# Places in the partition: moving and loaded operand trade places (byte 0 and 64 modulo 128) at every change of matrix behind the first network

## The chip, the cores and the metric

The kernel runs on one core of one Trainium2 chip, as one program. The metric is the device time of one execution in microseconds (us); smaller is better. Before the change it is 989.61 us, the median of three runs (989.24 to 990.04).

## The reference

A decoder trunk of two layers works on 256 positions of 1024 float32 features. Each layer is a mixer between two gated feed-forward networks, each on a normalised copy of x and added to x. The mixer of the first layer is a gated MLP with a causal 128 x 128 mix of positions; that of the second is stick-breaking attention, whose keys and values come from x as it is ahead of the second layer.

```python
def swiglu(h, w_in, w_out):
    gu = h @ w_in
    gate, up = jnp.split(gu, 2, axis=-1)
    return (jax.nn.silu(gate) * up) @ w_out

for i in range(DEPTH):                      # DEPTH = 2, N_A = 1
    if i == N_A:
        kv = rms_norm(x, kv_norm) @ w_kv    # shared keys and values
    x = x + 0.5 * swiglu(rms_norm(x, ffn_norm[i, 0]), ffn_w_in[i, 0], ffn_w_out[i, 0])
    h = rms_norm(x, mix_norm[i])
    if i < N_A:
        x = x + chunked_sgu(h, ...)         # (u * (W_s LN(v) + b)) W_out, with u, v = gelu(h W_in)
    else:
        x = x + stick_breaking_attention(h @ b_w_q, k, v) @ b_w_o
    x = x + 0.5 * swiglu(rms_norm(x, ffn_norm[i, 1]), ffn_w_in[i, 1], ffn_w_out[i, 1])
return rms_norm(x, final_norm)
```

The hidden width of a network is 2816, that of the gated MLP 2048; there are 16 heads of 64 and 4 heads of keys and values.

## The kernel before

x is kept transposed (xT: 128 features in the partitions, 8 chunks, 256 positions). Every float32 operand of a large product is split into two float32r tiles, a high part and the rest, and `mm3` makes a product out of three matmuls: rest of a with high of b, high of a with rest of b, high with high. In a matmul, a is the operand loaded into TensorE (128 columns) and b the one that moves through it (256 columns, in the last out step 512). Each of the three matmuls has its own weight load. In the rows a matmul reads `out<-tile,tile`; wlo and whi are the rest and the high part of a piece of weights, and so on with l and h.

The stages, by the names of their PSUM tiles in the profile:

- Networks a, b, c and d (`ffn_in`, `ffn`). An in step computes 256 gate columns (ga, gb, gc, gd) and 256 up columns (ua to ud) with the weights loaded and the normalised x moving (xnh, xnl); 96 matmuls. An out step adds 256 hidden features (hh, hl) into y (ya, yb, yc); 48 matmuls with the weights loaded and h moving. 11 in and 11 out steps stand in turn, an out step two behind its in step; one of each make a period of 144 matmuls. Network d's out step (yo with hhd) is turned round: h is loaded and the weights move, 512 columns at a time.
- Between a and b the gated MLP: v (`project_rows`: xn loaded, weights moving), then the u loop: uu (weights loaded, xn moving), mix, ys (weights loaded, hhs moving).
- Between b and c the keys (kT) and the values (v again, from xk). Between c and d the attention: q, z, the transposes at, o, and yo with oT moving.

The weights come in by DMA from SP's queue in pieces of 128 x 1024, up to seven ahead. ScalarE rounds a piece into whi (line 85) and VectorE writes the rest into wlo (line 87). The pools hip and lop hold nine tiles each. A tile has 1056 elements per partition (4224 bytes), of which a piece takes 1024, from element `place` on: `W.add(source, place)`. Place 16 is 64 bytes. No order is written out for the networks beyond the loops; `ATT_STEPS` sets that of the attention.

The pools stand one behind the other in each partition, so tile sizes decide addresses. xnh and xnl are neighbours of 8192 bytes each; hh and hl are pools of four tiles of 2048 bytes. The bytes modulo 128 at which the operands of a step start:

| step | moving / loaded before | after |
|---|---|---|
| in step of a | 0 / 64 | 0 / 64 |
| out step of a | 64 / 0 | 64 / 0 |
| v | 64 / 0 | 0 / 64 |
| uu, in steps of b, c, d, q | 0 / 64 | 64 / 0 |
| ys, out steps of b and c, yo with oT | 64 / 0 | 0 / 64 |
| kT; values (v from xk) | 64 / 64; 64 / 64 | 64 / 0; 0 / 64 |
| z | 0 / 64 | 0 / 64 |
| o | 64 / 0 | 64 / 0 |
| out step of d | 0 / 64 | 0 / 64 |

Of the kernel before, what the change touches and what calls it, by code (L numbers as in the profile page):

```python
# [9 lines left out]
F32R = mybir.dt.float32r  # L10
# [5 lines left out]
P = 128  # L16
T = 256
D = 1024
KC = D // P
DFF = 2816  # L20
NPAIR = DFF // 256
DA = 2048
# [81 lines left out]
def trunk(  # L104
# [22 lines left out]
    out = out[0]  # L127
# [8 lines left out]
    act = ctx.enter_context(tc.tile_pool(name="act", bufs=1))  # L136
# [5 lines left out]
    hp = ctx.enter_context(tc.tile_pool(name="hp", bufs=4))  # L142
# [8 lines left out]
    def ybank(name):  # L151
        return py.tile([P, 512], F32, tag="py", name=name)

    def scratch(name, width=512):
        return scr.tile([P, width], F32, tag="scr", name=name, padded_shape=[P, 516])

# [21 lines left out]
    W = Weights(tc, rawp, hip, lop)  # L178

    def cols(w, c0, kh):  # L180
        return w[kh * 512 : (kh + 1) * 512, c0 : c0 + 256].rearrange("(k p) c -> p k c", p=P)

    def rows(w, r0):
        return w[r0 : r0 + P, :]

    def plan_in_out(n, ins, w_out):


        steps = {}
        for j in range(n + 1):  # L190
            if j < n:
                steps["in", j] = [[W.add(cols(w, c0 + 256 * j, kh)) for w, c0 in ins] for kh in range(2)]
            if j:
                steps["out", j - 1] = [W.add(rows(w_out, 256 * (j - 1) + P * m), 16) for m in range(2)]
        return steps

    def plan_ffn(i, s):
        return plan_in_out(NPAIR, [(ffn_w_in[i, s], 0), (ffn_w_in[i, s], DFF)], ffn_w_out[i, s])

    plan00 = plan_ffn(0, 0)  # L200
    plan_v = [[W.add(cols(a_w_in[0], DA + 256 * j, kh)) for kh in range(2)] for j in range(8)]
    plan_u = {}
    for step in U_STEPS:
        kind, j = step
        if kind == "in":
            plan_u[step] = [W.add(cols(a_w_in[0], 256 * j, kh)) for kh in range(2)]
        elif kind == "out":
            plan_u[step] = [W.add(rows(a_w_out[0], 256 * j + P * m), 16) for m in range(2)]
    plan01 = plan_ffn(0, 1)
    plan_kv = [[W.add(cols(w_kv, 256 * j, kh)) for kh in range(2)] for j in range(2)]  # L210
    plan10 = plan_ffn(1, 0)
    plan_q = [[W.add(cols(b_w_q[0], 256 * j, kh)) for kh in range(2)] for j in range(4)]
    plan_o = [W.add(rows(b_w_o[0], P * b), 16) for b in range(8)]
    plan11 = plan_ffn(1, 1)


    xin = {}
# [17 lines left out]
    for i, group in enumerate(ROWS):  # L235
        r0 = 0
        for name, ap in group:
            n = ap.shape[0]
# [32 lines left out]


    xT = act.tile([P, KC, T], F32, name="xT")
    xnh = act.tile([P, KC, T], F32R, name="xnh")
    xnl = act.tile([P, KC, T], F32R, name="xnl")
    acc = act.tile([P, T], F32, name="acc")
    rT = act.tile([P, 2], F32, name="rT")

# [4 lines left out]
    def prepare(d, gains, sq=True):  # L283

        for (name, i), h, l in gains:
            g = gain(name, i * KC + d)
            W.order(nc.scalar.activation(h[:, d, :], xT[:, d, :], AF.Copy, scale=g))
            W.order(
                nc.vector.scalar_tensor_tensor(  # L289
                    l[:, d, :], xT[:, d, :], g, h[:, d, :].bitcast(F32), ALU.mult, ALU.subtract  # L290
                )
            )
        if sq:
            square(d)
# [49 lines left out]
    def load_x(hf):  # L344

        for d in range(hf * 4, hf * 4 + 4):
            ptr = ybank(f"ptr{d}")
            for tt in range(2):
                W.order(
                    nc.tensor.transpose(  # L350
                        ptr[:, tt * P : (tt + 1) * P], xin[tt, hf][:, (d % 4) * P : (d % 4 + 1) * P], ident
                    )
                )
            if d % 2:
                W.order(nc.vector.tensor_copy(xT[:, d, :], ptr[:, :T]))
            else:
                W.order(nc.scalar.copy(xT[:, d, :], ptr[:, :T]))
        for d in range(hf * 4, hf * 4 + 4):
            prepare(d, [(("ffn", 0), xnh, xnl)], False)
            if d % 2 == 0:  # L360
                s = scratch(f"sqx{d}", T) if d else acc
                nc.gpsimd.tensor_mul(s, xT[:, d, :], xT[:, d, :])
                if d:
                    nc.gpsimd.tensor_add(acc, acc, s)
            if d == 2:
                W.piece = 512
                W.run_to(0, 1)
                W.piece = UNIT
        W.run_to(0, 2)
        for d in range(hf * 4 + 1, hf * 4 + 4, 2):  # L370
            square(d)
# [81 lines left out]
            if kh + 1 in mid:  # L453
                mid[kh + 1]()

    XN = (xnh, xnl)

    def ffn_in(tag, j, ids, mid={}, by_bank=False):

        banks = [gbank(f"g{tag}_{j}"), gbank(f"u{tag}_{j}")]  # L460
        project(banks, ids, XN, mid, by_bank)
        gs = scratch(f"gs{tag}_{j}")
        us = scratch(f"us{tag}_{j}")
        nc.vector.tensor_mul(pair(gs), pair(banks[0]), bc2(rb))
        nc.scalar.activation(gs, gs, AF.Silu)
        nc.vector.tensor_mul(pair(us), pair(banks[1]), bc2(rb))
        nc.vector.tensor_mul(us, us, gs)
        hh = hp.tile([P, 512], F32R, tag="hh", name=f"hh{tag}_{j}")
        hl = hp.tile([P, 512], F32R, tag="hl", name=f"hl{tag}_{j}")
        split(hh, hl, us)  # L470
        return hh, hl

# [56 lines left out]
    def spatial_bias(hf):  # L529
# [13 lines left out]
    norm = Rms("x")  # L543
    ffn(
        "a",
        plan00,
        [(("mix", 0), xnh, xnl)],
        {1: lambda: load_x(1), 3: norm.columns, 4: norm.rows},
        True,
        {  # L550
# [22 lines left out]
    norm = Rms("m0")  # L573
# [30 lines left out]
    def mix(j, u):  # L604
        bank = gbank(f"mix{j}")
        s = scratch(f"mx{j}")
        for m in range(2):
            c = 2 * j + m
            for n in range(2):
                nc.tensor.matmul(  # L610
                    bank[:, m * T + n * P : m * T + (n + 1) * P],
                    vsb[:, n, c * P : (c + 1) * P],
                    wsT[:, j, :],
                    start=True,
                    stop=True,
                )
            nc.vector.scalar_tensor_tensor(
                s[:, m * T : (m + 1) * T].rearrange("p (n t) -> p n t", n=2),
                bank[:, m * T : (m + 1) * T].rearrange("p (n t) -> p n t", n=2),
                gain("lng", c),  # L620
                bc2(bias[:, c, :]),
                ALU.mult,
                ALU.add,
            )
        nc.vector.tensor_mul(s, s, u)
        hh = hp.tile([P, 512], F32R, tag="hh", name=f"hhs{j}")
        hl = hp.tile([P, 512], F32R, tag="hl", name=f"hls{j}")
        split(hh, hl, s)
        return hh, hl

# [2 lines left out]
    y = Residual("s")  # L633
    tail = []
    for kind, j in U_STEPS:
# [4 lines left out]
        else:  # L640
            h = hs.pop(j)
            for m in range(2):
# [2 lines left out]
                    y.add(w, chunk(h, m), j == 0 and m == 0, False)  # L645
                else:
                    tail.append((w, chunk(h, m)))
    close(y, tail, 0, 1.0, [(("ffn", 1), xnh, xnl)])
    sgu.close()


# [3 lines left out]
    kz = [at.tile([P, 4, 2, T], F32R, name=f"kz{p}") for p in "hl"]  # L655
    vd = [at.tile([P, 2, 4, 2, 64], F32R, name=f"vd{p}") for p in "hl"]
    at.tile([P, 16], F32, name="gapx")
    xkh = at.tile([P, KC, T], F32R, tag="bigh", name="xkh")
    xkl = at.tile([P, KC, T], F32R, tag="bigl", name="xkl")
    for t in kz:  # L660
        nc.gpsimd.memset(t.bitcast(F32), 0.0)

    norm = Rms("f1")
    ffn("b", plan01, [(("kv", 0), xkh, xkl), (("ffn", 2), xnh, xnl)], {1: norm.columns, 2: norm.rows})


    XK = (xkh, xkl)
    bank = gbank("kT")
    norm = Rms("f2")
    project([bank], [[i] for i in plan_kv[0]], XK, {2: norm.columns})  # L670
# [17 lines left out]
        for r in range(2):  # L688
            split(vd[0][:, tt, :, r, :], vd[1][:, tt, :, r, :], src)

    ffn("c", plan10, [(("mix", 1), xnh, xnl)])
    zscale = [at.tile([P, 2], F32, name=f"zscale{n}") for n in "pn"]
    oT = [at.tile([P, KC, T], F32R, tag=f"big{p}", name=f"oT{p}") for p in "hl"]

    def q_out(j, bank):
        qh = hp.tile([P, 512], F32R, tag="hh", name=f"qh{j}")
        ql = hp.tile([P, 512], F32R, tag="hl", name=f"ql{j}")
        split(qh, ql, bank)
        return qh, ql

# [49 lines left out]
    def transposed(b, a):  # L750
        t0 = gbank(f"at0_{b}")
        t1 = gbank(f"at1_{b}")
        for h in range(2):
            nc.tensor.transpose(t0[:, h * T : h * T + P], a[0][:, h, :], ident)
            nc.tensor.transpose(t0[:, h * T + P : (h + 1) * T], a[1][:, h, :P], ident)
            nc.tensor.transpose(t1[:, h * P : (h + 1) * P], a[1][:, h, P:], ident)
        a0 = [hp.tile([P, 512], F32R, tag=f"h{p}", name=f"a0{p}{b}") for p in "hl"]
        a1 = [hp.tile([P, T], F32R, tag=f"a1{p}", name=f"a1{p}{b}", bufs=2) for p in "hl"]
        split(a0[0], a0[1], t0)
        split(a1[0], a1[1], t1[:, :T])  # L760
        return a0, a1
# [27 lines left out]
    y = None  # L789
# [24 lines left out]
    for step in ATT_STEPS.split():  # L814
        if step == "y":
            y = Residual("o")
        else:
            att_step(step[0], int(step[1]))
    close(y, tail, 0, 1.0, [(("ffn", 3), xnh, xnl)])
    att.close()  # L820


# [103 lines left out]
```

## Time and profile before

| | |
|---|---|
| median of three runs | 989.61 us |
| the profiled execution's own time | 990.2 us |
| its span, first to last instruction | 988.5 us |
| TensorE busy | 970.1 us, 8042 matmuls |
| weight loads busy | 950.6 us |
| VectorE / ScalarE / GpSimd busy | 642.8 / 503.5 / 85.5 us |
| mean granted TensorE clock | 0.995 |

Matmuls are pipelined: the duration of one in the profile (some 278 ns) is longer than the distance between the starts of two, so the pace is read from the starts in the timeline. Over a longer stretch it is the first start of the stretch, the first start behind it, and the count between. Where TensorE is busy without a break, a stage's time is its count of matmuls times that distance.

### The profile page before, as it was taken

Reading aid. Unit: us, or ns where it says so; the run is one execution under the profiler, and the core shown is the slowest. Engines: PE = TensorE matmul, PEld = TensorE weight load, DVE = VectorE, ACT = ScalarE, POOL = GpSimd, SP = SyncE. Lnnn points to the kernel's source line nnn. Section 1 sums busy time; section 2 is a strip of 40 time slices with the busy share of each in tenths; the row PEclk is TensorE's granted clock in tenths of the full one; section 3 lists DMA queues with packets and bytes.
Section 4 is the critical chain, followed back from the end, with each engine's and each line's share of the span. In section 5 each row is a group of like instructions: output and inputs, shape, how many; then the busy total and the mean of one; then the engine's idle time right before and its main releaser. Section 6 shows DMA issues by size and latency. Waiting matters only on the chain.

```text
span 988.5 us, 19306 instructions
## 1 busy us (share of the span) xinstructions
PE 970.1 (98%) x8042; PEld 950.6 (96%) x8042; DVE 642.8 (65%) x823; ACT 503.5 (51%) x690; POOL 85.5 (9%) x126
## 2 busy tenths in 40 slices
PE   9999999999999999999999999999998999999997
PEld 8999999999999999999999999999997899999996
DVE  6865666676866775656569665656678776555553
ACT  6644434575544563434358444444587675343433
POOL 4100000010000300000003000000156320000002
PEclk9999999999999999999999999999999999999999
DMA  9966565657555466666664856565643246656511
GB/s 293 335 204 194 178 189 188 192 161 222 176 188 172 129 203 194 196 194 195 191 195 144 251 180 202 182 207 178 193 155 96 92 132 210 195 188 199 186 43 43
DMA packets 135208, 179.56 MB, mean 182 GB/s; under 512 B 5624, under 2 KB 119376, under 8 KB 135120
## 3 DMA queue, kind: packets, MB, share of 16 engines
q1 hardware_dynamic: 134768, 177.76, 57.8%
q8 instruction: 63, 1.03, 0.4%
q0 software_dynamic: 192, 0.52, 0.2%
q14 instruction: 25, 0.20, 0.1%
q10 hardware_dynamic: 160, 0.05, 0.0%
HBM read 176.73 MB, written 1.05 MB: 180 GB/s over the span
## 4 chain that ended last, share of the span: by engine, by line
PE 88%; DVE 5%; ACT 2%; issue 1%; DMA 1%; POOL 1%; SPq 0%; ACTq 0%; POOLq 0%; DVEq 0%
PE yo L160 2%; PE yo L162 2%; PE yo L161 2%; PE gc L162 2%; PE uc L162 2%; PE gb L160 2%; PE gc L161 2%; PE gc L160 2%; PE uc L161 2%; PE gb L162 2%; PE gb L161 2%; PE ub L162 2%; PE uc L160 2%; PE ub L161 2%; PE ub L160 2%; PE ud L162 2%
## 5 line engine op out<-in xcount | busy, mean ns | idle before, releaser
L85 ACT CAST whi<-raw 128x1024 fp32r<-128x1024 f32 (+1 forms) x333 | 342.4, 1044 | 379.1 <-issue 194.3
L87 DVE TENSOR_TENSOR wlo<-raw,whi 128x1024 fp32r<-128x1024 f32 (+1 forms) x333 | 401.6, 1223 | 193.9 <-ACT whi L85 193.0
L302 POOL TENSOR_TENSOR acc<-acc,sq 128x256 f32<-128x256 f32 x39 | 33.6, 863 | 378.2 <-ACT sq L301 376.3
L160 PE MATMUL ga<-xnh,wlo 128*128 128x256 f32 x176 | 49.9, 283 | 0.0
L160 PE MATMUL ua<-xnh,wlo 128*128 128x256 f32 x176 | 48.8, 277 | 0.5 <-DVE wlo L87 0.5
L161 PE MATMUL ga<-xnl,whi 128*128 128x256 f32 x176 | 49.1, 279 | 0.2 <-DVE xnl L289 0.2
L160 PE MATMUL ya<-hha,wlo 128*128 128x256 f32 x176 | 48.9, 278 | 0.2 <-DVE xT L411 0.2
L160 PE MATMUL yc<-hhc,wlo 128*128 128x256 f32 x176 | 48.9, 278 | 0.1
L160 PE MATMUL gb<-xnh,wlo 128*128 128x256 f32 x176 | 49.0, 278 | 0.0
L160 PE MATMUL gd<-xnh,wlo 128*128 128x256 f32 x176 | 48.9, 278 | 0.0
L160 PE MATMUL yb<-hhb,wlo 128*128 128x256 f32 x176 | 48.9, 278 | 0.0
L162 PE MATMUL ga<-xnh,whi 128*128 128x256 f32 x176 | 48.9, 278 | 0.0
L160 PE MATMUL gc<-xnh,wlo 128*128 128x256 f32 x176 | 48.9, 278 | 0.0
L162 PE MATMUL gc<-xnh,whi 128*128 128x256 f32 x176 | 48.8, 277 | 0.0
L162 PE MATMUL uc<-xnh,whi 128*128 128x256 f32 x176 | 48.8, 277 | 0.0
L161 PE MATMUL gc<-xnl,whi 128*128 128x256 f32 x176 | 48.7, 277 | 0.0
L162 PE MATMUL gd<-xnh,whi 128*128 128x256 f32 x176 | 48.7, 277 | 0.0
L162 PE MATMUL gb<-xnh,whi 128*128 128x256 f32 x176 | 48.7, 277 | 0.0
L162 PE MATMUL ud<-xnh,whi 128*128 128x256 f32 x176 | 48.7, 277 | 0.0
L161 PE MATMUL gb<-xnl,whi 128*128 128x256 f32 x176 | 48.7, 277 | 0.0
L162 PE MATMUL ua<-xnh,whi 128*128 128x256 f32 x176 | 48.7, 277 | 0.0
L161 PE MATMUL uc<-xnl,whi 128*128 128x256 f32 x176 | 48.7, 277 | 0.0
(289 smaller groups left out, 3345.3 us busy)
## 6 DMA issues: line engine op xcount, KB each, us to landing
raw<-in_ffn_w_in_dram SPq DMA_DIRECT2D x176, 512.0 KB, 4.7
raw<-in_ffn_w_out_dram SPq DMA_DIRECT2D x88, 512.0 KB, 4.2
raw<-in_a_w_in_dram SPq DMA_DIRECT2D x32, 512.0 KB, 4.5
raw<-in_a_w_out_dram SPq DMA_DIRECT2D x16, 512.0 KB, 3.3
raw<-in_b_w_q_dram SPq DMA_DIRECT2D x8, 512.0 KB, 4.6
raw<-in_b_w_o_dram SPq DMA_DIRECT2D x8, 512.0 KB, 4.1
raw<-in_w_kv_dram SPq DMA_DIRECT2D x4, 512.0 KB, 4.2
xin<-in_x_dram SPq DMA_DIRECT2D x4, 256.0 KB, 4.9
```

The costliest lines, as they stand in the source:

```text
L85: ins = nc.scalar.copy(hi[:, cc], raw[:, cc])
L87: ins = nc.vector.tensor_sub(lo[:, cc], raw[:, cc], hi[:, cc].bitcast(F32))
L160: nc.tensor.matmul(o, al, bh, start=first, stop=False, skip_group_check=True)
L161: nc.tensor.matmul(o, ah, bl, start=False, stop=False, skip_group_check=True)
L162: nc.tensor.matmul(o, ah, bh, start=False, stop=last, skip_group_check=True)
L302: nc.gpsimd.tensor_add(acc, acc, s)
```

## The change

Only the addresses of tiles change. Network a keeps its places. Behind it the weights of each matrix, and the operands that they meet, are placed so that a step's moving operand starts at the half (byte 0 or 64 modulo 128) at which the moving operand of the step before it did not; z, o and their neighbours excepted, as the table above shows. For this the tiles of xn, xk, oT and h get 32 elements (128 bytes) more, so that they can start at element 0 or 16: xnh and xnl, which `placed` cuts twice (XA for network a, XN behind it), xk and oT, and the h tiles that `hidden` hands out. So the distance from xnh to xnl goes from 8192 to 8320 bytes, those from xkh to xkl and from oTh to oTl likewise, and that between neighbouring h tiles from 2048 to 2176 bytes; from hh to hl of one step it is 8704 instead of 8192. All that lies behind moves along. No instruction is added, taken away or moved on any engine, and no wait.

```diff
+    def hidden(tag, name, n=0):
+
+        return hp.tile([P, 512 + 32], F32R, tag=tag, name=name)[:, n : n + 512]
...
-    def plan_in_out(n, ins, w_out):
+    def plan_in_out(n, ins, w_out, at_in, at_out):
...
-                steps["in", j] = [[W.add(cols(w, c0 + 256 * j, kh)) for w, c0 in ins] for kh in range(2)]
+                steps["in", j] = [[W.add(cols(w, c0 + 256 * j, kh), at_in) for w, c0 in ins] for kh in range(2)]
...
-                steps["out", j - 1] = [W.add(rows(w_out, 256 * (j - 1) + P * m), 16) for m in range(2)]
+                steps["out", j - 1] = [W.add(rows(w_out, 256 * (j - 1) + P * m), at_out) for m in range(2)]
...
+    plan00 = plan_ffn(0, 0, 0, 16)
+    plan_v = [[W.add(cols(a_w_in[0], DA + 256 * j, kh), 16) for kh in range(2)] for j in range(8)]
...
-            plan_u[step] = [W.add(cols(a_w_in[0], 256 * j, kh)) for kh in range(2)]
+            plan_u[step] = [W.add(cols(a_w_in[0], 256 * j, kh), 16) for kh in range(2)]
...
-            plan_u[step] = [W.add(rows(a_w_out[0], 256 * j + P * m), 16) for m in range(2)]
...
+            plan_u[step] = [W.add(rows(a_w_out[0], 256 * j + P * m)) for m in range(2)]
+    plan01 = plan_ffn(0, 1, 16, 0)
+    plan_kv = [[W.add(cols(w_kv, 256 * j, kh), 16) for kh in range(2)] for j in range(2)]
+    plan10 = plan_ffn(1, 0, 16, 0)
+    plan_q = [[W.add(cols(b_w_q[0], 256 * j, kh), 16) for kh in range(2)] for j in range(4)]
+    plan_o = [W.add(rows(b_w_o[0], P * b)) for b in range(8)]
+    plan11 = plan_ffn(1, 1, 16, 16)
...
-    xnh = act.tile([P, KC, T], F32R, name="xnh")
-    xnl = act.tile([P, KC, T], F32R, name="xnl")
+    xnb = [act.tile([P, KC * T + 32], F32R, name=f"xn{p}") for p in "hl"]
+
+    def placed(n, ts=xnb):
+
+        return tuple(t[:, n : n + KC * T].rearrange("p (k t) -> p k t", k=KC) for t in ts)
+
+    XA = placed(0)
+    XN = placed(16)
...
-        project(banks, ids, XN, mid, by_bank)
+        project(banks, ids, XA if tag == "a" else XN, mid, by_bank)
...
-        hh = hp.tile([P, 512], F32R, tag="hh", name=f"hh{tag}_{j}")
-        hl = hp.tile([P, 512], F32R, tag="hl", name=f"hl{tag}_{j}")
+        hh, hl = (hidden(f"h{p}", f"h{p}{tag}_{j}", 16 if tag in "bc" else 0) for p in "hl")
...
+        hh, hl = (hidden(f"h{p}", f"h{p}s{j}", 16) for p in "hl")
...
-    xkh = at.tile([P, KC, T], F32R, tag="bigh", name="xkh")
-    xkl = at.tile([P, KC, T], F32R, tag="bigl", name="xkl")
+    XK = placed(0, [at.tile([P, KC * T + 32], F32R, tag=f"big{p}", name=f"xk{p}") for p in "hl"])
...
-    oT = [at.tile([P, KC, T], F32R, tag=f"big{p}", name=f"oT{p}") for p in "hl"]
+    oT = placed(16, [at.tile([P, KC * T + 32], F32R, tag=f"big{p}", name=f"oT{p}") for p in "hl"])
...
+        qh, ql = (hidden(f"h{p}", f"q{p}{j}") for p in "hl")
...
-        a0 = [hp.tile([P, 512], F32R, tag=f"h{p}", name=f"a0{p}{b}") for p in "hl"]
+        a0 = [hidden(f"h{p}", f"a0{p}{b}") for p in "hl"]
```

## Rows read from the trace of the kernel before

**Rows 1.** The page: busy engines, granted clock by slices, chain by engine.
```profile
PE 970.1 (98%) x8042; PEld 950.6 (96%) x8042; DVE 642.8 (65%) x823; ACT 503.5 (51%) x690; POOL 85.5 (9%) x126
...
PEclk9999999999999999999999999999999999999999
...
PE 88%; DVE 5%; ACT 2%; issue 1%; DMA 1%; POOL 1%; SPq 0%; ACTq 0%; POOLq 0%; DVEq 0%
```

**Rows 2.** Windows by stage, all engines; the first line names the columns.
```profile
core 0: us, PE busy (x) PEld busy (x) DVE busy (x) ACT busy (x) POOL busy (x), PEclk, DMA share, GB/s
36.00:186.00 150.00, 150.00 (x1309) 148.85 (x1308) 94.14 (x112) 64.44 (x72) 0.00 (x0) 1.00 0.66 202
197.00:244.00 47.00, 46.84 (x398) 46.59 (x397) 31.53 (x47) 29.70 (x45) 4.95 (x5) 1.00 0.61 185
340.00:522.00 182.00, 182.00 (x1597) 181.79 (x1596) 114.14 (x137) 88.70 (x114) 6.55 (x9) 1.00 0.62 190
535.00:715.00 180.00, 180.00 (x1575) 179.78 (x1574) 113.09 (x127) 83.39 (x101) 4.16 (x9) 1.00 0.67 205
715.00:796.00 81.00, 73.25 (x547) 69.12 (x547) 63.84 (x95) 58.60 (x114) 36.62 (x63) 0.96 0.35 111
```

**Rows 3.** Timeline, TensorE: network a's change from in to out (start us, us).
```profile
136.77 0.28 PE L160 MATMUL ya<-hha,wlo 128*128 128x256 f32 x1
136.88 0.28 PE L161 MATMUL ya<-hla,whi 128*128 128x256 f32 x1
...
139.49 0.28 PE L160 MATMUL ya<-hha,wlo 128*128 128x256 f32 x1
```

**Rows 4.** Timeline, TensorE: the v projection around 216 us and its end.
```profile
215.83 0.28 PE L160 MATMUL v<-whi,xnl 128*128 128x256 f32 x1
...
216.17 0.28 PE L160 MATMUL v<-whi,xnl 128*128 128x256 f32 x1
216.29 0.28 PE L161 MATMUL v<-wlo,xnh 128*128 128x256 f32 x1
...
216.76 0.28 PE L162 MATMUL v<-whi,xnh 128*128 128x256 f32 x1
...
244.42 0.28 PE L160 MATMUL uu<-xnh,wlo 128*128 128x256 f32 x1
```

**Rows 5.** Timeline, TensorE: network a's change from out to in.
```profile
159.43 0.28 PE L160 MATMUL ga<-xnh,wlo 128*128 128x256 f32 x1
...
159.79 0.28 PE L160 MATMUL ga<-xnh,wlo 128*128 128x256 f32 x1
```

**Rows 6.** Timeline, TensorE: first matmuls of two in steps of network b.
```profile
369.42 0.28 PE L160 MATMUL gb<-xnh,wlo 128*128 128x256 f32 x1
...
500.32 0.28 PE L160 MATMUL gb<-xnh,wlo 128*128 128x256 f32 x1
```

**Rows 7.** Timeline, TensorE: starts in the in steps of network c.
```profile
563.05 0.28 PE L160 MATMUL gc<-xnh,wlo 128*128 128x256 f32 x1
...
568.75 0.28 PE L160 MATMUL gc<-xnh,wlo 128*128 128x256 f32 x1
...
694.64 0.28 PE L160 MATMUL gc<-xnh,wlo 128*128 128x256 f32 x1
```

**Rows 8.** Groups of matmuls by line and shape, TensorE.
```profile
L160 PE MATMUL ga<-xnh,wlo 128*128 128x256 f32 x176 | 49.9, 283 | 0.0
...
L160 PE MATMUL uu<-xnh,wlo 128*128 128x256 f32 x128 | 35.5, 277 | 0.0
...
L160 PE MATMUL yo<-oTh,wlo 128*128 128x256 f32 x64 | 18.4, 294 | 0.3
L160 PE MATMUL q<-xnh,wlo 128*128 128x256 f32 x64 | 17.9, 280 | 0.0
```

**Rows 9.** Timeline, TensorE: the last network's out step (512 columns).
```profile
838.13 0.39 PE L160 MATMUL yo<-whi,hld 128*128 128x512 f32 x1
...
840.90 0.39 PE L160 MATMUL yo<-whi,hld 128*128 128x512 f32 x1
```

More of the change, by code (lines that the diff above doesn't have):

```diff
@@ L191, in plan_in_out, with plan_ffn @@
             if j < n:
-                steps["in", j] = [[W.add(cols(w, c0 + 256 * j, kh)) for w, c0 in ins] for kh in range(2)]
+                steps["in", j] = [[W.add(cols(w, c0 + 256 * j, kh), at_in) for w, c0 in ins] for kh in range(2)]
             if j:
-                steps["out", j - 1] = [W.add(rows(w_out, 256 * (j - 1) + P * m), 16) for m in range(2)]
+                steps["out", j - 1] = [W.add(rows(w_out, 256 * (j - 1) + P * m), at_out) for m in range(2)]
         return steps
[L197 to L201, printed above, removed]
+    def plan_ffn(i, s, at_in, at_out):
+        return plan_in_out(
+            NPAIR, [(ffn_w_in[i, s], 0), (ffn_w_in[i, s], DFF)], ffn_w_out[i, s], at_in, at_out
+        )
+    plan00 = plan_ffn(0, 0, 0, 16)
+    plan_v = [[W.add(cols(a_w_in[0], DA + 256 * j, kh), 16) for kh in range(2)] for j in range(8)]
     plan_u = {}
@@ L205, in trunk @@
         if kind == "in":
-            plan_u[step] = [W.add(cols(a_w_in[0], 256 * j, kh)) for kh in range(2)]
+            plan_u[step] = [W.add(cols(a_w_in[0], 256 * j, kh), 16) for kh in range(2)]
         elif kind == "out":
-            plan_u[step] = [W.add(rows(a_w_out[0], 256 * j + P * m), 16) for m in range(2)]
[L209 to L214, printed above, removed]
+            plan_u[step] = [W.add(rows(a_w_out[0], 256 * j + P * m)) for m in range(2)]
[5 more added lines that the diff above has]
+    plan11 = plan_ffn(1, 1, 16, 16)
     xin = {}
@@ L358, in load_x @@
         for d in range(hf * 4, hf * 4 + 4):
-            prepare(d, [(("ffn", 0), xnh, xnl)], False)
+            prepare(d, [(("ffn", 0), *XA)], False)
             if d % 2 == 0:
@@ L454, in project_rows @@
                 mid[kh + 1]()
-    XN = (xnh, xnl)
     def ffn_in(tag, j, ids, mid={}, by_bank=False):
         banks = [gbank(f"g{tag}_{j}"), gbank(f"u{tag}_{j}")]
-        project(banks, ids, XN, mid, by_bank)
+        project(banks, ids, XA if tag == "a" else XN, mid, by_bank)
         gs = scratch(f"gs{tag}_{j}")
@@ L546, in trunk @@
         plan00,
-        [(("mix", 0), xnh, xnl)],
+        [(("mix", 0), *XN)],
         {1: lambda: load_x(1), 3: norm.columns, 4: norm.rows},
@@ L625, in mix @@
         nc.vector.tensor_mul(s, s, u)
-        hh = hp.tile([P, 512], F32R, tag="hh", name=f"hhs{j}")
-        hl = hp.tile([P, 512], F32R, tag="hl", name=f"hls{j}")
+        hh, hl = (hidden(f"h{p}", f"h{p}s{j}", 16) for p in "hl")
         split(hh, hl, s)
@@ L647, in trunk @@
                     tail.append((w, chunk(h, m)))
-    close(y, tail, 0, 1.0, [(("ffn", 1), xnh, xnl)])
+    close(y, tail, 0, 1.0, [(("ffn", 1), *XN)])
     sgu.close()
@@ L663, in trunk @@
     norm = Rms("f1")
-    ffn("b", plan01, [(("kv", 0), xkh, xkl), (("ffn", 2), xnh, xnl)], {1: norm.columns, 2: norm.rows})
-    XK = (xkh, xkl)
+    ffn("b", plan01, [(("kv", 0), *XK), (("ffn", 2), *XN)], {1: norm.columns, 2: norm.rows})
     bank = gbank("kT")
@@ L689, in trunk @@
             split(vd[0][:, tt, :, r, :], vd[1][:, tt, :, r, :], src)
-    ffn("c", plan10, [(("mix", 1), xnh, xnl)])
+    ffn("c", plan10, [(("mix", 1), *XN)])
     zscale = [at.tile([P, 2], F32, name=f"zscale{n}") for n in "pn"]
-    oT = [at.tile([P, KC, T], F32R, tag=f"big{p}", name=f"oT{p}") for p in "hl"]
+    oT = placed(16, [at.tile([P, KC * T + 32], F32R, tag=f"big{p}", name=f"oT{p}") for p in "hl"])
     def q_out(j, bank):
-        qh = hp.tile([P, 512], F32R, tag="hh", name=f"qh{j}")
-        ql = hp.tile([P, 512], F32R, tag="hl", name=f"ql{j}")
+        qh, ql = (hidden(f"h{p}", f"q{p}{j}") for p in "hl")
         split(qh, ql, bank)
@@ L818, in trunk @@
             att_step(step[0], int(step[1]))
-    close(y, tail, 0, 1.0, [(("ffn", 3), xnh, xnl)])
+    close(y, tail, 0, 1.0, [(("ffn", 3), *XN)])
     att.close()
```

## The prediction

> **What bounds the kernel now.** I read the busy shares first, then the stretches, then the timeline of single matmuls. TensorE is busy 98% of the 988.5 us, the chain that ended last is 88% TensorE, and its granted clock is 9 (90% or more) in every slice, so it stands at the upper of its two levels, 2.4 GHz [rows 1]. By stretch it is busy in all of networks a, b and c, and in 46.84 of 47.00 us of the v projection; the attention leaves idle time (busy 73.25 of 81.00 us) [rows 2]. In the networks a to c VectorE and ScalarE stand below 65% there and the DMA share at two thirds. So time is the number of matmuls times the distance from one start to the next, and a change of addresses can do only one thing that counts: alter that distance.
>
> The distance is not the same everywhere. A matmul of 256 columns and its weight load go in step, and the rows show two spacings at the same clock and shape. In the first network's out step, 24 matmuls from 136.77 to 139.49 us take 2.72 us, 113.3 ns each [rows 3]. In the v projection, 240 matmuls from 216.17 to 244.42 us take 28.25 us, 117.7 ns each [rows 4]. No wait shows in either. I call them the short and the long spacing. In network c, 48 matmuls from 563.05 to 568.75 take 118.75 ns each [rows 7]: long spacing with another pattern.
>
> **What switches between them.** I set the start addresses of the built program beside the starts in the timeline, modulo 256 bytes, and looked at each matmul that follows at least five short spacings. Where its moving operand goes on at the place where the last one started (difference 0), the short spacing stays, for thousands of matmuls, even when the loaded operand jumps by 128 at every third one. Where the moving operand jumps by +64 (every in-to-out change of networks a to c: xn at 128, h at 192), it stays too, 30 times of 30; [rows 3] show one. Where it jumps by -64 (out-to-in, 192 back to 128), the next distances are long at every such change; [rows 5] show one, three matmuls from 159.43 to 159.79, 120 ns each. It comes back after some 4 to 48 matmuls, at a change of loaded tile. Where it jumps by 128, the spacing goes long too: this happens from the first network into v and at 216.17 us, the only place where v had short spacing. There the moving operand goes from the whi tile to its wlo tile, 38016 bytes = 148.5 x 256 further, at 216.29; the three matmuls from 215.83 to 216.17 took 113 ns each, the four from 216.29 to 216.76 117.5 [rows 4]. In the v stage 12 of 16 pairs of weight tiles have this jump of 128 between hi and lo at two of every three matmuls, and none of the 12 holds the short spacing; in the last network's out step (weights moving too) 12 matmuls of 512 columns from 838.13 to 840.90 us take 230.8 ns each, above twice 113.3 = 226.7 [rows 9].
>
> **The change, part by part.** No instruction, wait or order changes on any engine; only addresses do.
>
> 1. *Trading the halves (byte 0 and 64).* Within each step moving and loaded operand stood 64 apart and still do. By itself this turns the sign of the jumps at stage borders, a matter of some matmuls per border. Bounds: nothing, to 41 borders (11+11+11 network steps, 8 of the u loop) x 12 matmuls x 4.4 ns = 2.2 us either way; I take 0.
>
> 2. *xn's two tiles get 32 elements more.* This is the part that I think counts. xnh and xnl stood 8192 bytes = 32 x 256 apart; now it is 8320 = 32.5 x 256. Every in-projection streams xnh, xnl, xnh (lines 160 to 162), so two of every three of its matmuls now start with the moving operand 128 off modulo 256. In the built program such jumps rise from 430 to 3795. It holds for network a too, though its places are untouched. To the engine this is what v has today: two jumps of 128 in each triple, with moving and loaded operand an odd multiple of 64 apart.
> Count: 8 x 176 + 128 + 64 per line, three lines: 4800 matmuls (gates, ups, uu, q) [rows 8]. Price: they now run at a mixture. Eight periods of network b (1152 matmuls, 369.42 to 500.32) take 113.63 ns per matmul [rows 6], eight of c 114.23 (563.05 to 694.64) [rows 7]; mean 113.93; with the out third of a period at 113.3, its in part stands at (3 x 113.93 - 113.3) / 2 = 114.25. If none keeps the short spacing, they go to between 117.7 (v) and 118.75 (c's long stretch, whose loaded operand jumps as here). I take the middle, 118.2: 4800 x 3.95 ns = +19.0 us; ends +16.6 and +21.6. No trace shows an in-projection with this jump, so the lower end for a partial effect stays open, below as a rival.
>
> 3. *oT and xk widen in the same way.* 192 matmuls of the attention's output projection [rows 8], 4.3 ns: +0.8 us; bounds 0 (they lie partly beside the attention's idle time [rows 2]) and 0.9. kT and the kv values, 96 matmuls, had both operands at the same half; now opposite, but with the jump: 0, bounds -0.4 to +0.1.
>
> 4. *h tiles widen by 128 bytes.* hh and hl of one step are 4 x 2176 = 34 x 256 apart, so the out steps get no jump inside. But they are now entered from an in step with long spacing. Bounds: 0 to all 1968 matmuls (33 network out steps and 8 of ys, 48 each) long, x 4.4 = +8.7 us. Every long stretch that I followed ended at a change of loaded tile (c's at 568.75 after 48; uu after 24), and half of the entries are now jumps of +64, the harmless kind; I take +2.5.
>
> 5. *v and the last network's out step* keep their moving jumps from hi to lo weights: 0; v's loaded xn now jumps too, 0 to 384 x 1.05 ns (118.75 against 117.7) = +0.4; I take 0.
>
> 6. *ScalarE, VectorE, DMA*: same shapes, same counts; covered by TensorE, which in the networks never waits for them.
>
> Sum: 19.0 + 0.8 + 2.5 = +22.3 us. The profiled execution took 990.2 us (span 988.5); 1012.5. The median of the three runs, 989.6, is 0.6 below it, so I predict **1012 us**.
>
> **A rule weighed.** The Trainium skill (SBUF — State Buffer, "Who interferes with whom") gives TensorE two independent SBUF read ports and says that it never waits on anyone; TensorE: Matmul & The Clock Gate, "Step-by-step: what each phase is for", says that loading the next weights takes no read bandwidth from the running matmul. By it places would not matter and the time would stay at 989.6. The trace disagrees already: 117.7 against 113.3 ns at the same shape and clock.
>
> **Rivals.**
> - *No effect* (989.6 +- 1): the spacing depends on something other than addresses, for instance on which operand is the weights; v is long because its weights move, and xn's jump is harmless. For it: of the v and kv stages with moving weights nearly all are long, and jump and role come together in this trace. Against it: the one short stretch in v broke at a jump, at 216.17, and the four tile pairs of v without a jump include the only short one. Chance 0.09.
> - *Trading cures* (faster): a change of place at every border resets the step. Then v (entered so far without a trade) falls to 113.3: 8 blocks of 48 x 4.4 ns = 1.7 us; kT and values 96 x 5 = 0.5; the last network's out step, some 240 x 4.1 = 1.0; together -3.2, 986.4. It decides from the first border, network a into v: starts 113.3 ns apart behind some 200 us show it. Against it: borders with a trade go long at -64 today, and uu, entered with a trade, began with 24 long ones. Chance 0.06.
> - *Partial*: the jump breaks the spacing, but in some tile pairs it comes back, as for the -64 kind; half of the in matmuls long: 4800 x 2 ns = +9.5, 1000. Chance 0.07.
> - *Forecast*: 0.78; its own range is 1006 (16.6 alone) to 1021 (21.6 + 0.9 + 8.7).
>
> **Numbers.** The range must hold 8 in 10: the forecast's own and the partial case (1000, with 2 us below it), 998 to 1021; I leave out no effect and the cure (0.15) and the tails. A measurement of this kernel tells about 0.2% (2 us) from no change. Slower: forecast and partial, 0.85. Same: no effect, and a third of the cure, 0.10. Faster: 0.05.
>
> **What would show it.** Right: in networks a to d the in matmuls start 117.7 to 119 ns apart from the first tile to the last, the mean duration in the rows of ga and uu rises from 277 to 283 ns [rows 8] to 280 or more, network a slows as well although its places are unchanged; a period of b (144 matmuls) takes 16.8 us or more against 16.36. v stays near 117.7. Wrong: gb and gc still at 113.3 behind an xnl matmul; then the jump of the moving operand is not the cause. If only b to d slow and a doesn't, it is the traded halves (part 1) and not the widening (part 2).

## The result and the profile after

The change makes the kernel slower, by 1.8%: 1007.58 us, median of 5 runs (1007.13 to 1009.30), against 989.54 us of the kernel before, timed beside it (5 runs, 989.24 to 990.04). The ratio is 1.0185, 95% interval 1.0173 to 1.0197. The profiled execution took 1009.3 us, its span is 1007.6. The forecast was 1012, with a range of 998 to 1021.

From the page after: busy engines, granted clock by slices, chain by engine; they answer to [rows 1].
```profile
PE 987.2 (98%) x8042; PEld 967.4 (96%) x8042; DVE 643.6 (64%) x823; ACT 503.6 (50%) x690; POOL 86.0 (9%) x126
...
PEclk9999999999999999999999999999999999999999
...
PE 89%; DVE 5%; ACT 2%; issue 1%; DMA 1%; POOL 1%; SPq 0%; ACTq 0%; POOLq 0%; DVEq 0%
```

Nothing in them looks like a new bottleneck. The matmuls are as many, VectorE and ScalarE have the same busy times within a microsecond, the clock stands at the same level, and the chain is TensorE's. Only TensorE's busy times have grown: the matmuls' from 970.1 to 987.2 us, the weight loads' from 950.6 to 967.4. The windows by stage (the first line names the columns; the limits moved along with the stages) answer to [rows 2]:
```profile
core 0: us, PE busy (x) PEld busy (x) DVE busy (x) ACT busy (x) POOL busy (x), PEclk, DMA share, GB/s
36.00:186.00 150.00, 150.00 (x1276) 148.85 (x1276) 92.27 (x110) 62.96 (x72) 0.00 (x0) 1.00 0.64 200
197.00:247.00 50.00, 49.85 (x422) 49.43 (x421) 34.48 (x55) 32.05 (x52) 6.59 (x7) 1.00 0.62 190
347.00:533.00 186.00, 186.00 (x1591) 185.80 (x1590) 113.59 (x136) 88.04 (x112) 5.72 (x7) 1.00 0.59 185
546.00:731.00 185.00, 185.00 (x1583) 184.81 (x1583) 114.16 (x130) 84.35 (x105) 5.09 (x11) 1.00 0.65 198
```

TensorE is busy without a break in networks a to c as before, but gets through fewer matmuls in the same time: in 150 us of network a 1276 where it was 1309. So the pace has to be read from single starts. Timeline of TensorE, network a, the change from an out to an in step (start and duration in us), beside [rows 5]:
```profile
180.37 0.28 PE L164 MATMUL ga<-xnh,wlo 128*128 128x256 f32 x1
180.49 0.28 PE L165 MATMUL ga<-xnl,whi 128*128 128x256 f32 x1
180.61 0.28 PE L166 MATMUL ga<-xnh,whi 128*128 128x256 f32 x1
180.72 0.28 PE L164 MATMUL ga<-xnh,wlo 128*128 128x256 f32 x1
```

Three matmuls take 0.35 us, 117 ns each, and unlike before this does not pass: here are the starts of one in step of network b, of its next out step and the next in step, and of the in step eight periods later; then two of network c that lie eight periods apart. They answer to [rows 6] and [rows 7].
```profile
375.69 0.28 PE L164 MATMUL gb<-xnh,wlo 128*128 128x256 f32 x1
...
387.00 0.28 PE L164 MATMUL yb<-hhb,wlo 128*128 128x256 f32 x1
...
392.57 0.28 PE L164 MATMUL gb<-xnh,wlo 128*128 128x256 f32 x1
...
510.17 0.28 PE L164 MATMUL gb<-xnh,wlo 128*128 128x256 f32 x1
...
574.10 0.28 PE L164 MATMUL gc<-xnh,wlo 128*128 128x256 f32 x1
...
708.47 0.28 PE L164 MATMUL gc<-xnh,wlo 128*128 128x256 f32 x1
```

The in step takes 11.31 us for 96 matmuls, 117.8 ns each; the out step 5.57 us for 48, 116.0 ns; eight periods (1152 matmuls) 134.48 us, 116.7 ns on average, where [rows 6] give 130.90 us and 113.6 ns; a period of 16.81 us, where the prediction asked for 16.8 or more. Network c takes 134.37 us. By groups of matmuls, to be held beside [rows 8]:
```profile
L164 PE MATMUL ga<-xnh,wlo 128*128 128x256 f32 x176 | 50.6, 287 | 1.2 <-DVE wlo L87 1.2
...
L164 PE MATMUL uu<-xnh,wlo 128*128 128x256 f32 x128 | 36.0, 281 | 0.0
...
L164 PE MATMUL yo<-oTh,wlo 128*128 128x256 f32 x64 | 18.8, 300 | 0.2
L164 PE MATMUL q<-xnh,wlo 128*128 128x256 f32 x64 | 18.3, 285 | 0.0
```

The mean duration went from 283 to 287 ns in ga, 277 to 281 in uu, 294 to 300 in yo, 280 to 285 in q. The v projection and the last network's out step (512 columns) hold their pace: 240 matmuls of v from 221.04 to 249.15 us take 117.1 ns each, and 12 matmuls of 512 columns from 855.26 to 858.03 us 230.8 ns, as in [rows 4] and [rows 9].
```profile
221.04 0.28 PE L166 MATMUL v<-whi,xnh 128*128 128x256 f32 x1
...
249.15 0.28 PE L166 MATMUL v<-whi,xnh 128*128 128x256 f32 x1
...
855.26 0.40 PE L164 MATMUL yo<-whi,hld 128*128 128x512 f32 x1
...
858.03 0.39 PE L164 MATMUL yo<-whi,hld 128*128 128x512 f32 x1
```

**Where the time went.** In both whole timelines I summed what each distance between two starts has above 113.33 ns (226.67 for 512 columns). Distances more than 15 ns above are counted as waits, in a line of their own. In us:

```
                                          before   after   difference
in steps, uu, q (4800 matmuls)              3.93   21.21      +17.28
out steps of a, b, c and ys (1968)          1.42    2.38       +0.96
yo (with oT and in network d)               1.37    2.02       +0.65
v, kT, z, o                                 2.42    2.22       -0.20
waits, all stages                                              +0.96
stages without float32r, edges                                 -0.6
sum; profiled executions, 990.2 and 1009.3                    +19.1
```

Nearly all of it lies in the in-projections, in all four networks. Network a is one of them: its operands start at the halves (byte 0 or 64 modulo 128) that they had, but xnl, which lies behind the wider xnh, moved by 128 bytes modulo 256 there too.

### The profile page after: what moved, and what is told of

It reads as the page before. It is cut to its first block, busy times and chain, and to the rows that moved or that the text cites. A ratio compares the mean times of both kernels' runs of the same rounds, so it can differ in the third digit from the quotient of the medians.

```text
span 1007.6 us, 19306 instructions
## 1 busy us (share of the span) xinstructions
PE 987.2 (98%) x8042; PEld 967.4 (96%) x8042; DVE 643.6 (64%) x823; ACT 503.6 (50%) x690; POOL 86.0 (9%) x126
## 4 chain that ended last, share of the span: by engine, by line
PE 89%; DVE 5%; ACT 2%; issue 1%; DMA 1%; POOL 1%; SPq 0%; ACTq 0%; POOLq 0%; DVEq 0%
PE yo L164 2%; PE yo L166 2%; PE yo L165 2%; PE gb L164 2%; PE gc L165 2%; PE gc L164 2%; PE uc L164 2%; PE gb L165 2%; PE ub L164 2%; PE ub L165 2%; PE gc L166 2%; PE gb L166 2%; PE uc L165 2%; PE ub L166 2%; PE uc L166 2%; PE ud L164 2%
## 5 line engine op out<-in xcount | busy, mean ns | idle before, releaser
L164 PE MATMUL ud<-xnh,wlo 128*128 128x256 f32 x176 | 49.4, 281 | 0.0
L164 PE MATMUL uc<-xnh,wlo 128*128 128x256 f32 x176 | 49.4, 281 | 0.0
L166 PE MATMUL ub<-xnh,whi 128*128 128x256 f32 x176 | 49.4, 280 | 0.0
L164 PE MATMUL ub<-xnh,wlo 128*128 128x256 f32 x176 | 49.4, 280 | 0.0
```

The costliest lines, as they stand in the source:

```text
L164: nc.tensor.matmul(o, al, bh, start=first, stop=False, skip_group_check=True)
L166: nc.tensor.matmul(o, ah, bh, start=False, stop=last, skip_group_check=True)
```

## Experiments

Throughout, a *jump* is the distance modulo 256 bytes from where one matmul's operand starts to where the next one's does; "moving" and "loaded" say which operand, and a *triple* is the three matmuls of one `mm3`. The places are those of the built programs; the traces show the starts. The table has the mean distances between starts (ns) in each run's profiled execution, of all matmuls of 256 columns, waits of over 15 ns left out; "in" and "out" are the steps of the networks, and v includes the values.

```
               us    in a  out a     v    uu    ys  in b out b  in c out c  in d
before       989.5  114.0  113.6 117.5 114.3 115.9 113.9 113.7 114.4 113.7 114.0
after       1007.6  117.8  114.2 117.2 117.7 114.5 117.8 114.9 117.8 114.6 117.8
apart128    1006.8  117.8  113.8 117.4 117.8 114.9 117.8 113.8 117.8 114.4 117.8
apart256     989.0  113.7  113.6 117.7 114.3 115.6 113.9 113.6 114.4 113.7 114.0
trade256     989.9  113.8  113.6 117.7 115.0 114.5 113.8 114.2 114.3 114.3 113.9
wpitch      1011.9  117.7  117.8 114.9 116.1 117.7 117.8 117.8 117.8 117.8 117.8
wpair128    1005.5  118.0  114.0 118.0 116.9 116.3 118.6 114.1 118.8 114.2 114.2
smooth      1011.8  113.8  113.6 117.4 118.8 117.7 118.6 118.7 118.9 118.7 118.6
noborder     987.3  113.9  113.5 117.5 114.2 115.0 113.6 113.5 113.3 113.5 114.0
alternate    994.6  113.9  117.6 117.9 115.2 114.7 113.6 117.5 113.5 117.3 114.0
best         985.6  113.6  113.6 114.0 114.0 115.6 113.4 113.4 113.3 113.4 113.6
```

**1. Only the distance, nothing traded (apart128).** The kernel before with 128 unused bytes behind each of xn's two tiles:

```diff
     xnh = act.tile([P, KC, T], F32R, name="xnh")
+    act.tile([P, 32], F32, name="gap1")
     xnl = act.tile([P, KC, T], F32R, name="xnl")
+    act.tile([P, 32], F32, name="gap2")
```

> The kernel before with 128 unused bytes between xnh and xnl and 128 behind xnl; every other operand keeps its place modulo 256, no half is traded, no other tile is wider. Theory of the jump (the moving operand's start modulo 256 against that of the matmul before sets the spacing): all in steps of a to d, uu and q go to 117.7 ns between starts, as in the changed kernel: 4800 x (117.7 - 114.15) = +17.0 us, with a further 0 to 1.5 us in the out steps behind them; 1007 us (1005 to 1009). Theory of the trade (the exchanged halves at the borders make the loss): nothing is traded, 989.5 +- 1.

Measured: 1006.75 us, ratio 1.0177 (1.0162 to 1.0193). Timeline: an in step of b, its out step, the next in step.
```profile
373.85 0.28 PE L160 MATMUL gb<-xnh,wlo 128*128 128x256 f32 x1
...
385.15 0.28 PE L160 MATMUL yb<-hhb,wlo 128*128 128x256 f32 x1
...
390.62 0.28 PE L160 MATMUL gb<-xnh,wlo 128*128 128x256 f32 x1
```

The in step takes 11.30 us (117.7 ns), the out step 5.47 (114.0). Of all operands xnl alone has another place modulo 256 (the second gap makes up a whole 256 for what lies behind), and that has nearly the whole effect of the change.

**2. The same with a whole 256 (apart256).**

```diff
+    act.tile([P, 64], F32, name="gap1")
     xnl = act.tile([P, KC, T], F32R, name="xnl")
```

> The kernel before with 256 unused bytes between xnh and xnl and none behind: the same total shift as in the run with 128, the distance now 33 x 256 bytes. Theory of the jump: no matmul's moving operand jumps that did not before, 989.5 +- 1, in matmuls at 113.3 to 114.5 ns. Rival that any distance other than 8192 bytes, or the moving along of the tiles behind, makes the loss: 1005 to 1009.

Measured: 989.0 us, ratio 0.9998 (0.9989 to 1.0007). Timeline: eight periods of b, by the first matmuls of two in steps.
```profile
367.79 0.28 PE L160 MATMUL gb<-xnh,wlo 128*128 128x256 f32 x1
...
498.69 0.28 PE L160 MATMUL gb<-xnh,wlo 128*128 128x256 f32 x1
```

130.90 us, as in [rows 6]. Neither the larger distance nor the shift of all that lies behind counts. Of the three distances tried, 8192 and 8448 bytes (multiples of 256) are fast and 8320 is slow; other remainders than 0 and 128 were not run.

**3. All trades, the distance a multiple of 256 (trade256).** The changed kernel with wider padding:

```diff
-        return hp.tile([P, 512 + 32], F32R, tag=tag, name=name)[:, n : n + 512]
+        return hp.tile([P, 512 + 64], F32R, tag=tag, name=name)[:, n : n + 512]
...
-    xnb = [act.tile([P, KC * T + 32], F32R, name=f"xn{p}") for p in "hl"]
+    xnb = [act.tile([P, KC * T + 64], F32R, name=f"xn{p}") for p in "hl"]
```

xk and oT likewise.

> The changed kernel with all its trades of halves, but the tiles of xn, xk, oT and h widened by 64 elements (256 bytes) where it has 32, so high and low part lie a multiple of 256 bytes apart. Theory of the jump: in steps back to 113.3 to 114.5 ns, the loss gone: 989.5 +- 2. Theory of the trade: the loss stays, 1007. Rival of the prediction that trading cures v, kT and the last network's out step once the jump is out of the way: 986.4; v would show it by 113.3 ns behind its first tiles; by the jump theory v stays at 117.7, since its weights still jump.

Measured: 989.94 us, ratio 1.0006 (0.9997 to 1.0015). Eight periods of b, by the first matmuls of two in steps:
```profile
368.81 0.28 PE L164 MATMUL gb<-xnh,wlo 128*128 128x256 f32 x1
...
500.06 0.28 PE L164 MATMUL gb<-xnh,wlo 128*128 128x256 f32 x1
```

131.25 us, 113.9 ns per matmul, against 130.90 in [rows 6]. Trading the halves by itself costs and gains nothing that can be measured; v, entered with a trade, stays at 117.7. That settles the change. The next runs ask what keeps a spacing.

**4. Weight tiles of 17 x 256 bytes (wpitch).** In the kernel before, wlo lies 148.5 x 256 bytes behind whi in most pairs, so v's moving weights jump. With 4352 bytes per tile, whi and wlo of every piece lie at one place modulo 256:

```diff
-                pool.tile([P, UNIT + 32], F32R, tag=f"w{p}", name=f"w{p}{i}")[:, self.places[i] : self.places[i] + UNIT]
+                pool.tile([P, UNIT + 64], F32R, tag=f"w{p}", name=f"w{p}{i}")[:, self.places[i] : self.places[i] + UNIT]
```

> The kernel before with weight tiles of 1088 elements (4352 = 17 x 256 bytes) in place of 1056 (4224 = 16.5 x 256), so that whi and wlo lie a multiple of 256 apart whatever slots they have; nothing else changes. Theory of the jump: v, whose moving operand is the weights, falls from 117.7 to between 113.3 and 114.5 ns: 384 x 3.2 to 4.4 ns = -1.2 to -1.7 us; the last network's out step, 512 columns, 0 to -1.0 us; 987.0 (986 to 988.5). Theory of the role (matmuls with weights moving are long because of that, not because of addresses): 989.5 +- 0.7, v stays at 117.7.

Measured: 1011.89 us, ratio 1.0229 (1.0215 to 1.0242). Timeline: 240 matmuls of v; then an in step of b, its out step and the next in step.
```profile
220.95 0.28 PE L162 MATMUL v<-whi,xnh 128*128 128x256 f32 x1
...
248.15 0.28 PE L162 MATMUL v<-whi,xnh 128*128 128x256 f32 x1
...
375.29 0.28 PE L160 MATMUL gb<-xnh,wlo 128*128 128x256 f32 x1
...
386.60 0.28 PE L160 MATMUL yb<-hhb,wlo 128*128 128x256 f32 x1
...
392.25 0.28 PE L160 MATMUL gb<-xnh,wlo 128*128 128x256 f32 x1
```

v did what was expected: from its fifth weight tile on it is short, here 27.20 us, 113.3 ns each, with the weights moving. So the role of the weights is not what makes v long. The total missed by 25 us: in and out steps of the networks stand at 117.7 to 117.8 ns from end to end (here 11.31 us and 5.65 us), though no operand jumps inside a step. The long spacing does not need a jump to go on. What the kernel before had and this one lacks is that neighbouring weight tiles lie 128 apart modulo 256 (4224 = 16.5 x 256).

**5. whi and wlo always 128 apart (wpair128).** On top of 4, to see whether a jump of the loaded operand inside each triple brings the short spacing back:

```diff
+    gap("gapl", 128)
     lop = ctx.enter_context(tc.tile_pool(name="lop", bufs=9))
...
-    gap("gaph", 128)
+    gap("gaph", 256)
```

> The run with weight tiles of 4352 bytes plus one gap of 128 bytes between the pools of whi and wlo (and 128 behind them), so that whi and wlo now always lie 128 apart modulo 256 instead of never; in the kernel before they do for most pairs. Theory, widened after the run with 4352 bytes: a jump of 128 of the moving operand ends the short spacing, a jump of 128 of the loaded operand brings it back, and where neither jumps the spacing stays what it was. Then the networks, whose loaded operand now jumps in every triple, return to 113.3 to 114 ns and lose the few long stretches of the kernel before (pairs that did not jump): 987.5 (986.5 to 989), 24 us under the run with 4352 bytes; v, whose moving weights jump in every pair, at 117.7. Rival that the pitch of 4352 itself is what costs (tiles all at one place): 1011.

Measured: 1005.52 us, ratio 1.0162 (1.0148 to 1.0176): in the in steps of a to c it does not, in the out steps (114.0 to 114.2 ns, 117.8 in run 4) and in network d (114.2) it does. Timeline, each time the first and the 85th matmul of an in step, of network c and of network d, and for c the out step between:
```profile
575.22 0.28 PE L161 MATMUL gc<-xnh,wlo 128*128 128x256 f32 x1
...
585.20 0.28 PE L161 MATMUL gc<-xnh,wlo 128*128 128x256 f32 x1
...
586.62 0.28 PE L161 MATMUL yc<-hhc,wlo 128*128 128x256 f32 x1
...
592.10 0.28 PE L161 MATMUL gc<-xnh,wlo 128*128 128x256 f32 x1
...
843.91 0.28 PE L161 MATMUL gd<-xnh,wlo 128*128 128x256 f32 x1
...
853.43 0.28 PE L161 MATMUL gd<-xnh,wlo 128*128 128x256 f32 x1
```

9.98 us for 84 matmuls in c, 118.8 ns; 9.52 in d, 113.3 ns. The operands of both have the same places modulo 256 and the same jumps inside the step. So either spacing can hold at one set of addresses, and which one is there depends on what ran before. In a to c each in step that follows an out step begins with a moving jump of -64 and is long to its end; the out step behind it is short after some six matmuls, inside its first loaded tile (5.48 us, 114.2 ns). Network d's in steps follow its turned-round out step.

**6. No moving jump between in and out steps (smooth).** On top of 5, h at xn's place modulo 256 and the weights of in and out steps at one place; v's weights with high part and rest at one place; xk and oT at the other half than their weights. The borders of v keep a jump: +64 from network a into it, -64 from it into the u loop. In part:

```diff
...
-    gap("gaph", 256)
+    gap("gaph", 192)
...
-        hh = hp.tile([P, 512], F32R, tag="hh", name=f"hh{tag}_{j}")
-        hl = hp.tile([P, 512], F32R, tag="hl", name=f"hl{tag}_{j}")
+        hh, hl = (hidden(f"h{p}", f"h{p}{tag}_{j}") for p in "hl")
...
-                steps["out", j - 1] = [W.add(rows(w_out, 256 * (j - 1) + P * m), 16) for m in range(2)]
+                steps["out", j - 1] = [W.add(rows(w_out, 256 * (j - 1) + P * m)) for m in range(2)]
...
```

> As the run with the gap between whi and wlo, and further: h at the place of xn modulo 256 (128) and the weights of out steps at that of the in steps (64 and 192), so that the moving operand never jumps between in and out steps of a, b and c; v's and the values' weights with whi and wlo at one place (192), so that v's moving operand does not jump either; xk and oT at the half opposite to their weights; q, a0 and a1 keep their half. Theory as widened: in steps lose the 4 to 48 long matmuls behind each out step, 113.3 to 113.6 ns throughout; v between 113.3 and 117.7 as e.g. 0.7 us instead of 1.8 of excess; together -4 to -6 us against before: 984.5 (983 to 986.5). Rival that jumps of 64 at the borders do not matter and only the loaded pairs do: 987.5, as the run before this one.

Measured: 1011.80 us, ratio 1.0235 (1.0216 to 1.0254). Network a was short throughout, b, c and d long throughout. Timeline, the first and the 85th matmul of an in step in a and in b:
```profile
158.47 0.28 PE L166 MATMUL ga<-xnh,wlo 128*128 128x256 f32 x1
...
167.99 0.28 PE L166 MATMUL ga<-xnh,wlo 128*128 128x256 f32 x1
...
371.64 0.28 PE L166 MATMUL gb<-xnh,wlo 128*128 128x256 f32 x1
...
381.63 0.28 PE L166 MATMUL gb<-xnh,wlo 128*128 128x256 f32 x1
```

113.3 and 118.9 ns at the same places. v stood at 117.4 ns, the u loop came out of it with the long spacing, and no network behind it got rid of it. So the long spacing doesn't need the border jumps of -64 to stay alive. kT, 118.6 ns before with both operands at one half, fell to 114.4; but the halves are not enough to explain that, since in run 9 they are the same as here and kT has 117.7.

**7. The same, neighbouring tiles still 128 apart (noborder).** As 6, but on the kernel before, with its weight tiles of 4224 bytes; v is left as it was. In part:

```diff
...
-    gap("gaph", 128)
+    gap("gaph", 64)
...
-        hh = hp.tile([P, 512], F32R, tag="hh", name=f"hh{tag}_{j}")
-        hl = hp.tile([P, 512], F32R, tag="hl", name=f"hl{tag}_{j}")
+        hh, hl = (hidden(f"h{p}", f"h{p}{tag}_{j}") for p in "hl")
...
```

> The kernel before, with h moved to xn's place modulo 256 and the out steps' weights to element 0, so that the moving operand no longer jumps by -64 or +64 at the changes between in and out steps; the weight tiles keep their 4224 bytes, so neighbouring tiles still lie 128 apart. If the -64 jumps start the long stretches that the kernel before still has in its in steps (3.9 us over 113.33 ns per matmul in all), most of that goes: gb, gc and uc at 113.3 to 113.5 from end to end, time 986 to 987. Rival (long stretches come by themselves or from the loaded operand): in steps as before, 989 +- 1.

Measured: 987.25 us, ratio 0.9982 (0.9973 to 0.9991). Eight periods of network b, then of c, by the first matmuls of two in steps each:
```profile
368.10 0.28 PE L165 MATMUL gb<-xnh,wlo 128*128 128x256 f32 x1
...
498.65 0.28 PE L165 MATMUL gb<-xnh,wlo 128*128 128x256 f32 x1
...
561.26 0.28 PE L165 MATMUL gc<-xnh,wlo 128*128 128x256 f32 x1
...
691.82 0.28 PE L165 MATMUL gc<-xnh,wlo 128*128 128x256 f32 x1
```

130.55 and 130.56 us, 113.3 ns per matmul from end to end; [rows 7] have 131.59 us for c. So the jumps between in and out steps do start most of the long stretches that networks a to c had: from 36 us on, what these networks have above 113.33 ns fell from 2.6 to 0.7 us. Of all in steps' 3.93 us, 2.3 stay; they lie in the first steps of a and b, the u loop, q and network d.

**8. Wide weight tiles, places alternating (alternate).** wpitch with one more line: every second piece starts 128 bytes further into its tile.

```diff
-        self.places.append(place)
+        self.places.append(place + 32 * (len(self.sources) % 2))
```

> The kernel with weight tiles of 4352 bytes (17 x 256), in which every in and out step of the networks stayed at 117.8 ns, with one change: every second piece of weights starts 128 bytes further into its tile, so that the loaded operand changes by 128 modulo 256 from one tile to the next, as it does in the kernel before; whi and wlo of a piece still lie at the same place, and the moving operand does not jump within a step. Theory (a change of place in the loaded operand between tiles brings the short spacing back): in and out steps of networks a to c at 113.3 to 114.5 ns, time 987 to 990. Rivals: the pitch of 4352 bytes itself costs, or the long spacing once entered stays whatever the loaded operand does: 117.8 ns throughout, time 1009 to 1013.

Measured: 994.62 us, ratio 1.0054 (1.0042 to 1.0067), between the two forecasts. Timeline: an in step of b, its out step, the next in step.
```profile
370.89 0.28 PE L160 MATMUL gb<-xnh,wlo 128*128 128x256 f32 x1
...
381.79 0.28 PE L160 MATMUL yb<-hhb,wlo 128*128 128x256 f32 x1
...
387.44 0.28 PE L160 MATMUL gb<-xnh,wlo 128*128 128x256 f32 x1
```

The in step is short again, 10.90 us, 113.5 ns, after at most a few long distances; so a tile of 4352 bytes costs nothing in itself, and changes of place in the loaded operand do end the long spacing. But every out step is now long, 5.65 us, 117.7 ns, both tiles of it. It is entered by a moving jump of +64, which in the kernel before was harmless 30 times of 30. Whether the spacing is long behind such a jump depends on the loaded operand too: three of those 30 borders have the very places of this run's (moving 128 to 192, loaded 64 to 0), and behind them the distances were 113 to 114 ns again from the second matmul on. There the loaded operand then jumps by 128 in every triple; here high part and rest lie at one place. The one change of place inside an out step, after 24 of its 48 matmuls, does not end the long spacing.

**9. Both together (best).** noborder with wide weight tiles whose places alternate where weights are loaded, and stay in v and the values, where they move; v's moving operand does not jump then. In part, against the kernel before:

```diff
...
-    def add(self, source, place=0):
+    def add(self, source, place=0, alt=True):
...
-        self.places.append(place)
+        self.places.append(place + (32 * (len(self.sources) % 2) if alt else 0))
...
-    plan_v = [[W.add(cols(a_w_in[0], DA + 256 * j, kh)) for kh in range(2)] for j in range(8)]
+    plan_v = [[W.add(cols(a_w_in[0], DA + 256 * j, kh), alt=False) for kh in range(2)] for j in range(8)]
...
```

> Both together: no jump of the moving operand at the changes between in and out steps, weight tiles of 4352 bytes whose places alternate by 128 where weights are loaded, and do not where they move (v), so that v's moving operand does not jump either. If both readings hold: in and out steps of the networks and most of v at 113.3, time 984 to 986, faster than both kernels. If an entered long spacing stays: 1008 or more.

Measured: 985.63 us, ratio to the kernel before 0.9963 (0.9950 to 0.9975): the fastest of all. Timeline: 240 matmuls of v, eight periods of b.
```profile
214.29 0.28 PE L167 MATMUL v<-whi,xnh 128*128 128x256 f32 x1
...
241.49 0.28 PE L167 MATMUL v<-whi,xnh 128*128 128x256 f32 x1
...
366.32 0.28 PE L165 MATMUL gb<-xnh,wlo 128*128 128x256 f32 x1
...
496.88 0.28 PE L165 MATMUL gb<-xnh,wlo 128*128 128x256 f32 x1
```

27.20 us for v, 113.3 ns, where the kernel before had 28.25 ([rows 4]) and the kernel after 28.11; 130.56 us for eight periods of b.

## Why the prediction was right, and where its sizes were off

**What bounds the kernel, and what switches.** Right. Addresses alone moved the time, through the distance between matmuls, at a constant clock. apart128 and apart256 together show the cause: 128 bytes modulo 256 between the two moving tiles cost 1.8%, 256 bytes nothing.

**Part 2, the widening of xn.** The right term, a little too dear: +17.3 us measured, +19.0 predicted. The step that was off is the price. No in step held the short spacing, as supposed, but the long one came out at 117.75 ns on average (21.21 us above 113.33 ns, over 4800 matmuls), which is v's value and the lower end that I gave, and not at the middle, 118.2; network c's 118.75 pattern is not what a moving jump makes (wpair128 and smooth show it, with loaded jumps and no moving ones). And it was measured from 114.15 ns before (3.93 us over 4800 matmuls), not 114.25. 4800 x 3.6 = 17.3.

**Part 4, the out steps.** +0.96 us instead of +2.5. They did get longer behind long in steps (ya, yb and yc by 0.31, 0.66 and 0.51 us), but ys came down by 0.52, which I had not foreseen. trade256 shows the same, ys at 114.5 instead of 115.9 ns; but apart128, which trades nothing, has 114.9, so the cause of this part stays open.

**Part 3, oT and xk.** +0.6 us for yo with oT, +0.8 predicted; kT -0.05. **Part 1, the trade:** 0 predicted, and trade256 measures 1.0006, its interval through 1. **Part 5, v and the last out step:** 0 predicted; -0.13 us and nothing that shows. **Part 6:** VectorE's and ScalarE's busy times are unchanged.

The terms together gave 22.3 us, the trace 19.1. The traced execution is the slowest of the five, with 1.3 us more waits in network a's gates and ups than the trace of before; the median rose by 18.0.

**The rivals.** *No effect* fell with the result; its reason, that moving weights make v long, fell with wpitch, where v runs at 113.3 ns with the weights moving. *Trading cures* fell with trade256: behind the first border with a trade v stands at 117.7. *Partial* fell with the timelines: no in step holds the short spacing.

**Two reads.** apart128, two unused gaps of 128 bytes and the same instructions, costs 17.5 us. The Trainium skill (SBUF — State Buffer, "Who interferes with whom") lists TensorE's two reads as independent. By it, as the prediction put it, places would not matter; the 17.5 us say that they do. They don't say that the two reads disturb each other: a read could also depend on where its own last one started, and no run separates the two. Which part of the chip makes two addresses 128 apart cost more, no run here shows either.

**What stays open.** My picture in the prediction, that a jump breaks the spacing and a change of loaded tile restores it, was enough for this change and too simple beyond it. The runs show: with a moving jump of 128 in each triple no in step was short; without one, either spacing held for hundreds of matmuls at the same places (wpair128, smooth); loaded jumps inside each triple end the long one in wpair128's out steps, but not in its in steps of a to c nor in smooth; tiles whose places alternate end it in the in steps (alternate against wpitch, and best), but not in alternate's out steps. A rule that tells from the addresses which jump breaks and which restores, I don't have; the sign of a 64-byte jump is not it.

## What to carry to other kernels

Where TensorE is busy without a break and does one load per matmul, read the starts, not the busy share: two spacings at one clock are a sign that addresses count. Keep the parts of a moving operand that alternate from matmul to matmul a multiple of 256 bytes apart, padding included: in this kernel 128 bytes of padding cost 1.8%, and 256 nothing. After a change of any tile's size, check the starts in every stage, since a stage can inherit the slow spacing from the one before it.

## What the runs showed that I had not expected

- Both spacings hold themselves: 113.3 and 117.7 to 118.9 ns per load and matmul of 256 columns, at the same addresses modulo 256, clock and shapes, for hundreds of matmuls (smooth: network a short, b to d long).
- Weight tiles that all lie at one place modulo 256 cost 22.6 us (1011.89 against 989.25 beside it): the kernel before owes its time in part to a tile size of 16.5 x 256 bytes, which puts neighbouring tiles 128 apart.
- Places alone span 26 us, 985.6 to 1011.9, with the same instructions in the same order.
